# A router taken by token halves, with its products in column groups, two slots given new tenants, and three places reordered

## The chip, the cores and the metric

One core of one Trainium2 chip runs the kernel in one launch. The metric is device microseconds of one execution, the median of several. Before the change it is 545.25 us.

## The reference, cut to what matters

One encoder layer over 256 tokens of width 1024, batch 1, all in fp32:

```python
h = rmsnorm(x, g_mix)
rq, rk, rv, rg, nq, nk, nv, xq, gate_logits = split(h @ w_in)
y_ret = retention(rope(rq), rope(rk), rv, rg) @ w_ret_o
y_na  = neighbourhood_attention(nq, nk, nv, rpb) @ w_na_o
y_xa  = cross_attention(xq, rmsnorm(mem, g_mem) @ w_mem_kv) @ w_xa_o
x = x + (g_ret * y_ret + g_na * y_na + g_xa * y_xa) @ w_out
t = rmsnorm(x, g_ffn)
group  = top1(softmax(t @ w_router_group + b))          # 4 groups
expert = top2(softmax(t @ w_router_expert + b)[group])  # 4 experts in each
x = x + sum over the 2 chosen experts: weight * (silu(t @ w_gate) * (t @ w_up)) @ w_down
return rmsnorm(x, g_final)
```

There are 16 experts of hidden width 512. Each has 6.3 MB of weights, so their weights are most of what the kernel reads.

## The kernel before, in words

Tokens stand in two halves of 128 (index `a`), the width in eight blocks of 128 or two halves of 512 (index `n`). The big projections are three products each: a weight block is loaded raw, ScalarE casts it to a high part (L128) and VectorE subtracts to get a low part (L129), and TensorE adds hi*hi, hi*lo and lo*hi (L306 to L308 for token-major output, L288 to L290 for the transposed one, L874 to L876 in `wout`). The high and low parts live in the slots `h0` to `h4`. SyncE issues the loads in order; a load into a slot waits for the slot's last reader.

Up to the retention branch's output a scheduler sets the order of the work, except for instructions that `pin` keeps in program order. From there on (`tc.manual_schedule()`) the order is the program's.

Four stages matter here.

*The first row scaling.* `diag_of(col_x)` (L231 to L235) puts each token's factor on the diagonal of two 128x128 blocks on VectorE (L234). `row_of` (L237) multiplies that by ones on TensorE (L239) and copies it out (L241). The queries of the cross attention (`pair_T`, L396) read it.

*Rotation and neighbourhood attention.* `rope_T` (L538) multiplies the projection by cosines and sines and adds (L551), for two pairs of blocks. `na_probs` (L521) transposes the softmaxed scores (`flip`), then copies one half to SBUF on ScalarE (L524) and one on VectorE (L525). `na_out` (L528) multiplies these probabilities with the values (L533) on TensorE. `na_scores`, `na_probs` and `na_out` are called for four pairs of heads, between the projections for retention. Four GpSimd products (L582) that build the retention's decay matrix fall between the first two calls; ScalarE's exponentials (L581) feed them.

*The router*, from the second half of `wout`'s products to the first expert matmul. `x1_sum` (L883) adds the residual on VectorE, `x1_sq` squares it on ScalarE, `x1_T` (L892) transposes it, `x1_ev` (L895) copies that to SBUF. `logits` (L900) multiplies each transposed block, as the stationary operand, with 32 columns of `wr`. `seed` (L906) is a product of the identity with x1: it puts x1 into the four PSUM banks in which the experts' outputs are summed. `route` (L1011 to L1038) is a row of small VectorE operations: top group, top two experts, and `msk`, a 0/1 row of 16 for each token. Products with a triangle and with ones (L1054) count the tokens ahead of each token, `posm` (L1056, L1067) is a token's place in an expert's list, and `X` (L1108) compares that with 0 to 63 to make a 0/1 selection. `gather` (L1123) multiplies the normed x1, in a high part (`normed_hi`, L979) and a low part (`normed_lo`, L983), with `X`. The result is scaled into `xg` by ScalarE (L1146) and VectorE (L1150). `x1` and `xg` share slot `C1`, `x1_hi` is in `C2`. The two halves `a` go through this together: `route(0)` and `route(1)` are interleaved, and products follow when both are done.

*The experts*, in pairs: gate and up products (L1191) are written 64 columns wide, two experts side by side; then come the down products (L1210) and a scatter back to the tokens. `fetch(tag)` (L139) issues the next expert load of a fixed list into a slot that has come free.

Of the kernel before, what the change touches and what calls it, by code (L numbers as in the profile page):

```python
# [18 lines left out]
P = 128  # L19
# [11 lines left out]
def hybrid_encoder_kernel(  # L31
# [506 lines left out]
    def rope_T(tag, pts):  # L538
        hi, lo = [t.rearrange("p (c t) -> p c t", c=4) for t in pair(tag)]
        for b in range(2):  # L540
            cs = slice(2 * b, 2 * b + 2)
            u = by_row(cos, pts[b])
            v = small_tmp([P, 2, T])
            for d in (0, 64):
                V.tensor_tensor(
                    v[d : d + 64],
                    pts[b][64 - d : 128 - d],
                    sin[64 - d : 128 - d].unsqueeze(1).to_broadcast([64, 2, T]),
                    op=ALU.mult,
                )  # L550
            V.tensor_add(u, u, v)  # L551
            split(hi[:, cs], lo[:, cs], u)
        return hi, lo
# [16 lines left out]
    rk_hi, rk_lo = rope_T("C1", proj_T(units_T(W, C_RK, D), hT_hi, hT_lo))  # L570
    ps = na_probs(p)
# [192 lines left out]
    def expert_units():  # L764
# [39 lines left out]
        ("F", slot("F", [P, 4, 512])),  # L804
# [41 lines left out]
    for u in range(2):  # L846
# [15 lines left out]
        for _ in range(2 - u):  # L862
            lead_lo()
    A.activation(warm, mg[1][:, 1, 1, 511:512], AF.Exp)
# [3 lines left out]
    def wout(q, pts):  # L868
        w = halves.pop(0)
        for a in range(2):  # L870
            ts = slice(a * P, (a + 1) * P)
            for k in range(2):
                kk = 2 * q + k
                PE.matmul(pts[a], m_hi[kk // 4][:, kk % 4, ts], w[k][0], start=kk == 0, stop=False)  # L874
                PE.matmul(pts[a], m_hi[kk // 4][:, kk % 4, ts], w[k][1], start=False, stop=False)
                PE.matmul(pts[a], m_lo[kk // 4][:, kk % 4, ts], w[k][0], start=False, stop=kk == KT - 1)  # L876
        if not parts:
            hl_tags.remove(w[2])
            fetch(w[2])
# [22 lines left out]
    acc = [[None, None], [None, None]]  # L902

    def seed(base, a, n):
        acc[a][n] = acc[a][n] or pj([P, 512])
        PE.matmul(acc[a][n], ident, base[:, a, n * 512 : n * 512 + 512], start=True, stop=False)  # L906

    x1 = slot("C1", [P, 2, D])
    p0 = [pj([P, 512]) for _ in range(2)]
    for q in range(4):  # L910
        if q < 2:
            mt = mixed_T(1, q)
        wout(q, p0)
        if q < 2:
            mixed(1, q, mt)
        feed()
# [6 lines left out]
    rlog = [bank([P, 32]) for _ in range(2)]  # L923
    p1 = [pj([P, 512]) for _ in range(2)]
    xt = [bank([P, 4, P]) for _ in range(2)]
    x1T[0] = tmp([P, 4, 256])
    x1_sum(0, 0, p0)
    x1_sum(0, 1, p0)
    x1_sq(0, 0)
    x1_sq(0, 1)  # L930
    wout(0, p1)
    feed()
    wout(1, p1)
    fetch("A0")
    x1_T(0, 0, xt[0])
    x1_T(0, 1, xt[1])
    feed()
    x1_ev(0, 0, xt[0])
    x1_ev(0, 1, xt[1])
    wout(2, p1)  # L940
    logits(0, 0)
    logits(0, 1)
    feed()
    wout(3, p1)
    xt = [pj([P, 4, P]) for _ in range(2)]
    x1T[1] = tmp([P, 4, 256])
# [7 lines left out]
    x1_sum(1, 0, p1)  # L954
    fetch("E0")
    x1_T(1, 0, xt[0])
    x1_sq(1, 0)
    x1_ev(1, 0, xt[0])
    x1_sum(1, 1, p1)
    x1_rstd(0)  # L960
    x1_T(1, 1, xt[1])
    logits(1, 0)
    x1_sq(1, 1)
    x1_ev(1, 1, xt[1])
    logits(1, 1)
    x1_rstd(1)
    tx.close()
    tpx.close()
    fp = ctx.enter_context(tc.tile_pool(name="fp", bufs=1))
    for tag in ("T0", "T1"):  # L970
        home[tag] = fp
        fetch(tag)

    x1_hi = slot("C2", [P, 2, D], F32R)
# [12 lines left out]
    for a in range(2):  # L987
        for n in range(2):
            normed_hi(a, n)
            seed(x1, a, n)  # L990
    show("x1", x1)
# [19 lines left out]
    def route(a):  # L1011
        V.scalar_tensor_tensor(lgt[:, a, 0:20], rlog[a][:, :20], r2[:, a : a + 1], rb, op0=ALU.mult, op1=ALU.add)
        yield
        V.max(gval[:, a], lgt[:, a, 16:24])
        yield
# [3 lines left out]
        yield  # L1019
# [6 lines left out]
        yield  # L1026
        V.tensor_reduce(pad[:, a, 0:4], sel[:, a].rearrange("p g e -> p e g"), axis=AX.X, op=ALU.add)
        yield
        V.max(eval_[:, a], pad[:, a])
        yield  # L1030
        V.max_index(eidx[:, a], eval_[:, a], pad[:, a])
        yield
        for i in range(2):
            V.tensor_tensor(oh[:, i, a], io4, eidx[:, a, i : i + 1].to_broadcast([P, 4]), op=ALU.is_equal)
        yield
        V.tensor_add(m4[:, a], oh[:, 0, a], oh[:, 1, a])
        yield
        spread(msk, m4, a)  # L1038
        yield

    rt = [route(a) for a in range(2)]
    for i in range(16):
        if i < 11:
            next(rt[0])
        if i >= 5:
            next(rt[1])
    pp = bank([P, 3, 16])
    for o, pieces in (
        (pp[:, 0], ((tri, 0),)),
        (pp[:, 1], ((tri, 1), (ones, 0))),  # L1050
        (pp[:, 2], ((ones, 0), (ones, 1))),
    ):
        for i, (l, a) in enumerate(pieces):
            PE.matmul(o, l, msk[:, a], start=i == 0, stop=i == len(pieces) - 1)  # L1054
    posm = cp.tile([P, 2, 16], F32, name="posm")
    V.tensor_scalar(posm, msk, 1e6, -1e6, op0=ALU.mult, op1=ALU.add)  # L1056
    gneg = tiny(2, tag="gneg")
    V.tensor_scalar_mul(gneg, gval[:, :, 0], -1.0)
    gsum = tiny(2, tag="gsum")
# [3 lines left out]
    e21 = tiny(2, tag="e21")  # L1063
    V.tensor_sub(e21, eval_[:, :, 1], eval_[:, :, 0])
    A.activation(e21, e21, AF.Exp)
    A.activation(warm, e21[:, 0:1], AF.Silu)
    V.tensor_add(posm, posm, pp[:, 0:2])  # L1067
    cmax = tiny(1, tag="cmax")

    def counts():  # L1070
        V.tensor_reduce(cmax, pp[:, 2], axis=AX.X, op=ALU.max)

# [30 lines left out]
    counts()  # L1103

    def select(g):
        pd = slot("X", [P, 2, 4, SLOTS], F32R)
        for a in range(2):
            V.tensor_tensor(  # L1108
                pd[:, a],
                posm[:, a, 4 * g : 4 * g + 4].unsqueeze(2).to_broadcast([P, 4, SLOTS]),  # L1110
                iota.unsqueeze(1).to_broadcast([P, 4, SLOTS]),
                op=ALU.is_equal,
            )
        return pd

    def gather(pd, lead=False):
        pts = [bank([P, 2, 256]) for _ in range(4)]

        def part(u, x, first):
            for j in range(2):  # L1120
                ks = slice((2 * u + j) * P, (2 * u + j + 1) * P)
                for a in range(2):
                    PE.matmul(  # L1123
                        pts[u][:, j],
                        x[:, a, ks],
                        pd[:, a].rearrange("p e s -> p (e s)"),
                        start=first and j + a == 0,
                        stop=not first and j + a == 2,
                    )

        if lead:
            for u in range(4):
                part(u, x1_hi, True)
            for n in range(2):
                for a in range(2):
                    normed_lo(a, n)
        xg = slot("C1", [P, KT, 4, SLOTS])
        for u in range(4):
            pt = pts[u]
            if not lead:  # L1140
                part(u, x1_hi, True)
            part(u, x1_lo, False)
            if u % 2:
# [142 lines left out]
    def experts(pd, first, lead=False):  # L1286
# [19 lines left out]
        xg = gather(pd, lead)  # L1306
        for p in range(NP):
# [33 lines left out]
    pd0 = select(0)  # L1341
    experts(pd0, weights, True)
# [83 lines left out]
```

## Time and profile before

| | |
|---|---|
| median of 3 runs | 545.25 us (545.08 to 545.47) |
| the profiled execution | 545.44 us, its span 543.5 us |
| granted clock, mean | 0.994 of full speed |
| TensorE (PE) busy | 97% of the span |
| VectorE (DVE), ScalarE (ACT), GpSimd (POOL) | 49%, 42%, 3% |
| moved by DMA | 159.91 MB, mean 294 GB/s |

Times in rows are us from the span's start. A timeline row reads: start, length, engine, line, operation, output <- input, tile used by a matmul, shape, count of instructions in the row, and in square brackets the idle time before it with what ended it. Matmuls overlap their ends: the step from one to the next is the cost, the length is not (a 512-column record of L874 to L876 is 0.39 us long and follows the one before by 0.23 us). An fp32 matmul can be two records.

### The profile page before, as it was taken

Reading aid. Unit: us, or ns where it says so; the run is one execution under the profiler, and the core shown is the slowest. Engines: PE = TensorE matmul, PEld = TensorE weight load, DVE = VectorE, ACT = ScalarE, POOL = GpSimd, SP = SyncE. Lnnn points to the kernel's source line nnn. Section 1 sums busy time; section 2 is a strip of 40 time slices with the busy share of each in tenths; the row PEclk is TensorE's granted clock in tenths of the full one; section 3 lists DMA queues with packets and bytes.
Section 4 is the critical chain, followed back from the end, with each engine's and each line's share of the span. In section 5 each row is a group of like instructions: output and inputs, shape, how many; then the busy total and the mean of one; then the engine's idle time right before and its main releaser. Section 6 shows DMA issues by size and latency. Waiting matters only on the chain. (4 is left out here: it accounts for less than half of the span.)

```text
span 543.5 us, 7482 instructions
## 1 busy us (share of the span) xinstructions
PE 528.5 (97%) x2912; PEld 359.9 (66%) x2912; DVE 264.3 (49%) x461; ACT 229.0 (42%) x378; POOL 18.5 (3%) x21
## 2 busy tenths in 40 slices
PE   8999999999999999999999999999999999999992
PEld 6999899967778888888888863353435343534340
DVE  6598798995657768384566171130112111210122
ACT  6775566698654464544535261121111111111123
POOL 0005000040000000000000000000000000000000
PEclk9999999999999999999999999999999999999997
DMA  8987778045445799739983799999999999999962
GB/s 302 390 316 233 224 147 256 17 156 163 148 154 189 235 334 301 257 103 403 354 318 151 275 344 330 416 406 418 406 414 409 409 413 407 416 406 418 406 242 81
DMA packets 89815, 159.91 MB, mean 294 GB/s; under 512 B 13104, under 2 KB 27824, under 8 KB 89776
## 3 DMA queue, kind: packets, MB, share of 16 engines
q1 hardware_dynamic: 89056, 158.80, 80.1%
q10 hardware_dynamic: 720, 0.58, 0.3%
q8 instruction: 25, 0.41, 0.3%
q14 instruction: 14, 0.11, 0.1%
HBM read 158.32 MB, written 1.05 MB: 293 GB/s over the span
## 5 line engine op out<-in xcount | busy, mean ns | idle before, releaser
L129 DVE TENSOR_TENSOR h<-r,h 128x1024 fp32r<-128x1024 f32 x58 | 71.2, 1239 | 31.6 <-ACT h L128 31.2
L128 ACT CAST h<-r 128x1024 fp32r<-128x1024 f32 x58 | 60.2, 1048 | 23.4 <-PE pj L308 12.5
L306 PE MATMUL pj<-h,A 128*128 128x512 f32 x160 | 63.1, 394 | 0.0
L308 PE MATMUL pj<-h,A 128*128 128x512 f32 x160 | 62.7, 392 | 0.0
L307 PE MATMUL pj<-h,A 128*128 128x512 f32 x160 | 62.6, 391 | 0.0
L1199 DVE TENSOR_TENSOR gs<-gs,b 64x512 f32<-64x512 f32 x16 | 11.1, 691 | 87.1 <-ACT gs L1198 87.1
L288 PE MATMUL pj<-A,h 128*128 128x256 f32 x160 | 45.7, 286 | 0.0
L290 PE MATMUL pj<-A,h 128*128 128x256 f32 x160 | 45.5, 284 | 0.0
L289 PE MATMUL pj<-A,h 128*128 128x256 f32 x160 | 45.3, 283 | 0.0
L308 PEld LDWEIGHTS pj<-h,A 128*128 128x128 f32 x160 | 30.1, 188 | 6.9 <-issue 0.8
L306 PEld LDWEIGHTS pj<-h,A 128*128 128x128 f32 x160 | 30.1, 188 | 6.7 <-issue 0.4
L307 PEld LDWEIGHTS pj<-h,A 128*128 128x128 f32 x160 | 30.1, 188 | 6.3 <-DVE h L129 0.4
L1230 DVE SCALAR_TENSOR_TENSOR os<-b,c,os 128x512 fp32r<-128x512 f32 x16 | 12.0, 751 | 41.9 <-ACT os L1229 41.0
L1198 ACT ACTIVATE gs<-b 64x512 f32<-64x512 f32 x16 | 9.4, 588 | 51.8 <-PE b L1191 51.8
L288 PEld LDWEIGHTS pj<-A,h 128*128 128x128 f32 x160 | 30.7, 192 | 0.1
L290 PEld LDWEIGHTS pj<-A,h 128*128 128x128 f32 x160 | 30.7, 192 | 0.1
L289 PEld LDWEIGHTS pj<-A,h 128*128 128x128 f32 x160 | 30.7, 192 | 0.1
L129 DVE TENSOR_TENSOR h<-G,h 128x1024 fp32r<-128x1024 f32 x18 | 24.1, 1346 | 10.3 <-ACT h L128 9.8
L1229 ACT ACTIVATE os<-b,c 128x512 fp32r<-128x512 f32 x16 | 11.0, 687 | 40.6 <-PE b L1210 39.7
L1191 PE MATMUL b<-h,C 128*64 128x512 f32 x104 | 24.0, 592 | 0.0
L128 ACT CAST h<-G 128x1024 fp32r<-128x1024 f32 x18 | 18.8, 1049 | 10.6 <-PE pj L308 9.3
L1210 PE MATMUL b<-h,hh 128*64 128x512 f32 x64 | 21.3, 592 | 0.0
(327 smaller groups left out, 1029.3 us busy)
## 6 DMA issues: line engine op xcount, KB each, us to landing
r<-in_w_in_dram SPq DMA_DIRECT2D x20, 1024.0 KB, 5.4
h<-in_w_exp_down_dram SPq DMA_DIRECT2D x10, 1024.0 KB, 11.5
h<-in_w_exp_gate_dram SPq DMA_DIRECT2D x13, 512.0 KB, 11.0
h<-in_w_exp_up_dram SPq DMA_DIRECT2D x13, 512.0 KB, 11.1
r<-in_w_exp_down_dram SPq DMA_DIRECT2D x6, 1024.0 KB, 11.6
A<-in_w_exp_down_dram SPq DMA_DIRECT2D x5, 1024.0 KB, 11.4
r<-in_w_exp_gate_dram SPq DMA_DIRECT2D x9, 512.0 KB, 10.2
r<-in_w_exp_up_dram SPq DMA_DIRECT2D x9, 512.0 KB, 10.3
```

What stands on the lines that cost most here:

```text
L128: pin(A.copy(hi, part))
L129: pin(V.tensor_sub(lo, part, hi.bitcast(F32)))
L288: PE.matmul(pt, whi[:, cs], thi[:, k], start=k == 0, stop=False)
L289: PE.matmul(pt, whi[:, cs], tlo[:, k], start=False, stop=False)
L290: PE.matmul(pt, wlo[:, cs], thi[:, k], start=False, stop=k == kn - 1)
L306: PE.matmul(pts[a], thi[:, kk, ts], whi, start=first, stop=False)
L307: PE.matmul(pts[a], thi[:, kk, ts], wlo, start=False, stop=False)
L308: PE.matmul(pts[a], tlo[:, kk, ts], whi, start=False, stop=last)
L1191: PE.matmul(pt[c * 64 : c * 64 + 64], xg[:, k, p % 2 * 2 + i], w[:, 2 * c + j], start=k == 0, stop=k == KT - 1)
L1199: V.tensor_mul(gs[i * 64 : i * 64 + 64], gs[64:128], pt[64:128])
L1210: PE.matmul(pts[n][i * 64 : i * 64 + 64], hh[:, 2 * u + k], ws[i][1][:, k, ns], start=u + k == 0, stop=u + k == 2)
L1230: V.scalar_tensor_tensor(o[:, 1], pt, c, o[:, 0].bitcast(F32), op0=ALU.mult, op1=ALU.subtract)
```

## The change

It does five things. (1) `diag_of(col_x)` is called before the neighbourhood queries' weights are split, no longer inside the call of `row_of`. (2) `rope_T` of the keys takes a function that is called ahead of its last addition: the copies of the first `na_probs` come before that addition. (3) The router works on token half 0 while half 1's `wout` products still run. Its logits turn the operands around: `wr` (32 columns) is stationary, four blocks go to four groups of 32 output partitions, ScalarE copies the 128 rows (`sheaves`) and a product with `four` (four stacked 32x32 identities) adds the four groups. Seeds and the parts of the first gather are written out one by one between the waits; seeds are 256 columns wide. `x1_sq`, `normed_hi` and `normed_lo` come earlier; the three small products of the counts are split. The pieces of the gather's results that go to ScalarE and to VectorE are swapped for this first gather. (4) `x1` and the first `xg` live in slot `F`, `x1_hi` in a half-weight slot. `C1` and `C2` take the two expert loads that `F` and that half-weight slot took, right after the retention's output. (5) The order of VectorE's and ScalarE's work follows from (1) to (3).

```diff
+    diag_x = diag_of(col_x)
     nq_u = units_T(W, C_NQ, D, pin)
-    row_x = row_of("q", diag_of(col_x))
+    row_x = row_of("q", diag_x)
...
-            V.tensor_add(u, u, v)
+            if b and mid:
+                mid()
+                pin(V.tensor_add(u, u, v))
+            else:
+                V.tensor_add(u, u, v)
...
-    rk_hi, rk_lo = rope_T("C1", proj_T(units_T(W, C_RK, D), hT_hi, hT_lo))
-    ps = na_probs(p)
+    rk_hi, rk_lo = rope_T("C1", proj_T(units_T(W, C_RK, D), hT_hi, hT_lo), lambda: probs.append(na_probs(p)))
+    (ps,) = probs
...
-        ("F", slot("F", [P, 4, 512])),
+        ("", slot("F", [P, 4, 512])),
...
+    for tag in ("C1", "C2"):
+        fetch(tag)
     A.activation(warm, mg[1][:, 1, 1, 511:512], AF.Exp)
...
-            PE.matmul(rlog[a], x1T[n][:, j, a * P : (a + 1) * P], wr[:, k], start=k == 0, stop=k == KT - 1)
+            PE.matmul(
+                sheaf[a][32 * j : 32 * j + 32],
+                wr[:, k],
+                x1T[n][:, j, a * P : (a + 1) * P],
+                start=not n,
+                stop=bool(n),
+            )
+    def bound(a):
+        A.copy(sheaves[:, a], sheaf[a])
+        PE.matmul(rlog[a], sheaves[:, a], four, start=True, stop=True)
-    x1 = slot("C1", [P, 2, D])
+    x1 = slot("F", [P, 2, D])
...
+    wout(1, p1, ws[1], 0)
+    for a in range(2):
+        x1_T(0, a, xt[a])
+        x1_ev(0, a, xt[a])
+    wout(2, p1, ws[2], 0)
+    wout(3, p1, ws[3], 0)
+    for a in range(2):
+        logits(0, a)
+    x1_sum(1, 0, p1)
+    x1_sq(1, 0)
+    x1_rstd(0)
+    wout(1, p1, ws[1], 1)
+    used(ws[1])
+    fetch("A0")
+    x1_T(1, 0, xt[2])
+    x1_ev(1, 0, xt[2])
+    for n in range(2):
+        normed_hi(0, n)
+        normed_lo(0, n)
+    wout(2, p1, ws[2], 1)
+    used(ws[2])
+    logits(1, 0)
+    wout(3, p1, ws[3], 1, (0,))
+    bound(0)
+    wout(3, p1, ws[3], 1, (1,))
+    used(ws[3])
+    fetch("E0")
+    rt = [route(a) for a in range(2)]
+    next(rt[0])
+    x1_sum(1, 1, p1)
+    x1_sq(1, 1)
+    next(rt[0])
+    x1_rstd(1)
+    seed(x1, 0, 0)
+    x1_T(1, 1, xt[1])
+    x1_ev(1, 1, xt[1])
+    seed(x1, 1, 0)
+    logits(1, 1)
+    PE.matmul(pp[0], tri, msk[:, 0], start=True, stop=True)
+    pd0 = slot("X", [P, 2, 4, SLOTS], F32R)
+    settled(0)
+    chosen(pd0, 0, 0)
+    bound(1)
...
+    for u in range(3):
+        for x in (x1_hi, x1_lo):
+            part(lead[u], u, x, pd0, 0, x is x1_hi, False)
+    for n in range(2):
+        normed_hi(1, n)
+    for _ in range(2):
+        next(rt[1])
+    seed(x1, 0, 1)
...
+    settled(1)
+    counts()
+    chosen(pd0, 0, 1)
+    seed(x1, 1, 1, (0,))
+    part(spare, 3, x1_hi, pd0, 0, True, False)
+    part(spare, 3, x1_lo, pd0, 0, False, False)
+    for u in range(4):
+        part(lead[u], u, x1_hi, pd0, 1, False, False)
...
+    for n in range(2):
+        normed_lo(1, n)
+    for u in range(4):
+        part(lead[u], u, x1_lo, pd0, 1, False, True)
+    seed(x1, 1, 1, (1,))
```

`settled(a)` is the place of a half's tokens, `chosen(pd, g, a)` the 0/1 selection of a half, and `part` one block pair of the gather for one half and one of the two parts.

How the order moves is seen in three places. ScalarE's queue around the second call of `na_out`, before (`h_198` is the high part of a weight block for the retention's values, `t_170` the probabilities that the second `na_out` reads, `G_154` and `C_140` parts of the values and the keys, `t_151` the softmaxed scores):

```order
L128 CAST h_182_1518<-r_181_1516 128x1024
L354 ACTIVATE t_151_1350,sm_1349<-t_148_1342,mx_1343 128x256 x4
L316 ACTIVATE G_154_1368<-pj_1403,col_239 128x512
L358 ACTIVATE t_151_1350<-t_151_1350,rs_1355 128x256 x4
L128 CAST h_183_1521<-r_181_1516 128x1024
L316 ACTIVATE G_154_1368<-pj_1404,col_239 128x512
L524 COPY t_170_1466<-at_1457 128x512
L128 CAST h_198_1633<-r_197_1631 128x1024
L313 CAST B_108_994<-at_1501 128x256
```

And in the changed kernel:

```order
L354 ACTIVATE t_151_1350,sm_1349<-t_148_1342,mx_1343 128x256 x4
L128 CAST h_182_1518<-r_181_1516 128x1024
L358 ACTIVATE t_151_1350<-t_151_1350,rs_1355 128x256 x4
L316 ACTIVATE G_154_1368<-pj_1403,col_239 128x512
L128 CAST h_183_1521<-r_181_1516 128x1024
L316 ACTIVATE G_154_1368<-pj_1404,col_239 128x512
L128 CAST h_198_1633<-r_197_1631 128x1024
L525 COPY t_170_1466<-at_1457 128x512
L313 CAST B_108_994<-at_1501 128x256
```

The copy of the probabilities (L524 before, L525 now) now stands behind the cast of `h_198`. On VectorE the same holds: the subtraction of `h_198` now stands ahead of the other half's copy, where it stood ten instructions behind it. In the changed kernel's TensorE queue the second `na_out` stands four projection matmuls later.

TensorE's queue behind the last `wout` product, before (`C_359` is x1, `pj_2946` and `pj_2947` its transposes, `b_2855` and `b_2856` the logits of the halves):

```order
L892 MATMUL pj_2946<-ident,C_359_2771 128x128 x4
L892 MATMUL pj_2947<-ident,C_359_2771 128x128 x4
L900 MATMUL b_2855<-wr,t_385_2948 128x32 x4
L900 MATMUL b_2856<-wr,t_385_2948 128x32 x4
L906 MATMUL pj_2997<-C_359_2771,ident 128x512
L906 MATMUL pj_3000<-C_359_2771,ident 128x512
L906 MATMUL pj_3003<-C_359_2771,ident 128x512
L906 MATMUL pj_3006<-C_359_2771,ident 128x512
```

And in the changed kernel, where `F_2776` is x1, `X_3025` the selection, `h_382` and `E_378` the high and low part, and `b_2857` to `b_2860` the four banks `lead`:

```order
L955 MATMUL pj_2777<-F_2776,ident 128x256 x2
L899 MATMUL b_2858<-ident,F_2776 128x128 x4
L955 MATMUL pj_2778<-F_2776,ident 128x256 x2
L907 MATMUL b_2860<-t_377_2870,wr 32x128 x4
L1097 LDWEIGHTS tri
L1097 MATMUL b_2857<-msk,tri 128x16
L917 MATMUL b_2860<-four,sheaves 128x32
L1036 MATMUL b_2857<-X_3025,h_382_2904 128x256 x2
L1036 MATMUL b_2857<-X_3025,E_378_2872 128x256 x2
L1036 MATMUL b_2858<-X_3025,h_382_2904 128x256 x2
L1036 MATMUL b_2858<-X_3025,E_378_2872 128x256 x2
L1036 MATMUL b_2859<-X_3025,h_382_2904 128x256 x2
```

Seeds, the transposes of the last quarter of x1, its logits, the first count and parts of the gather now take turns; before, all seeds stood ahead of the counts, and the gather behind them. The last half-seed (`seed(x1, 1, 1, (1,))`) is TensorE's last product ahead of the experts, and the scaling of `xg`, which overwrites x1's slot, waits for it.

SyncE's queue of expert loads behind the first eight, before:

```order
L152 DMA B_480_3481<-in_w_exp_down_dram 128x2x1024
L152 DMA F_3487<-in_w_exp_down_dram 128x2x1024
L152 DMA h_483_3496<-in_w_exp_gate_dram 128x2x512
L152 DMA h_483_3496<-in_w_exp_up_dram 128x2x512
```

And in the changed kernel:

```order
L152 DMA B_469_3485<-in_w_exp_down_dram 128x2x1024
L152 DMA C_470_3491<-in_w_exp_down_dram 128x2x1024
L152 DMA C_472_3500<-in_w_exp_gate_dram 128x2x512
L152 DMA C_472_3500<-in_w_exp_up_dram 128x2x512
```

The list of loads is the same. The fourth of a row of down loads goes to `C` in place of `F`, and the gate and up load behind it to `C` in place of a half-weight slot; both are issued when the retention's output is done, where the second was issued in the middle of the router before.

## Rows read from the trace of the kernel before

**Rows 1.** The page's busy times: us, share of the span, instructions

```profile
PE 528.5 (97%) x2912; PEld 359.9 (66%) x2912; DVE 264.3 (49%) x461; ACT 229.0 (42%) x378; POOL 18.5 (3%) x21
```

**Rows 2.** TensorE's waits: line, releaser, us in total, times, longest

```profile
PE at L533 <- DVE t L525: 1.6, 3, 1.0
```

**Rows 3.** Busy us of PE, PEld, DVE, ACT, POOL; clock; DMA share, GB/s

```profile
285.00:300.00 15.00, 15.00 (x72) 12.40 (x71) 10.50 (x13) 8.70 (x11) 0.00 (x0) 1.00 0.38 140
325.00:330.00 5.00, 5.00 (x26) 1.68 (x24) 0.00 (x0) 0.42 (x2) 0.00 (x0) 1.00 0.62 214
330.00:524.00 194.00, 194.00 (x1014) 80.15 (x1012) 31.01 (x65) 32.56 (x61) 0.00 (x0) 1.00 1.04 409
524.00:528.00 4.00, 4.00 (x20) 1.79 (x17) 1.98 (x3) 1.55 (x3) 0.00 (x0) 1.00 0.14 53
```

**Rows 4.** Timeline, TensorE then VectorE, around the first row scaling

```profile
30.13 0.28 PE L290 MATMUL pj<-A,h 128*128 128x256 f32 x1
30.49 0.70 PE L239 MATMUL at<-t,ones_f 128*128 128x256 f32 x2
...
25.29 4.76 DVE L129 TENSOR_TENSOR h<-r,h 128x1024 fp32r<-128x1024 f32 x4 [0.91 <-ACT h L128]
29.96 0.47 DVE L234 TENSOR_SCALAR t<-ident,col 128x128 f32<-128x128 f32 x2
```

**Rows 5.** Timeline: PE, VectorE, ScalarE, GpSimd around the first na_out

```profile
115.26 1.08 PE L533 MATMUL at<-t,E 128*64 128x256 f32 x8 [1.04 <-DVE t L525]
...
112.82 1.78 DVE L551 TENSOR_TENSOR t<-t,t 128x512 f32<-128x512 f32 x1
114.53 0.68 DVE L525 COPY t<-at 128x512 f32<-128x512 f32 x1
...
112.97 0.56 ACT L524 COPY t<-at 128x512 f32<-128x512 f32 x1
...
112.52 3.21 POOL L582 TENSOR_TENSOR C<-C,t 128x512 f32<-128x512 f32 x2 [63.46 <-ACT t L581]
```

**Rows 6.** Timeline: ScalarE, VectorE, TensorE around the second na_out

```profile
125.70 0.57 ACT L524 COPY t<-at 128x512 f32<-128x512 f32 x1
126.17 1.06 ACT L128 CAST h<-r 128x1024 fp32r<-128x1024 f32 x1
...
127.05 0.68 DVE L525 COPY t<-at 128x512 f32<-128x512 f32 x1
...
127.79 1.08 PE L533 MATMUL at<-t,E 128*64 128x256 f32 x8 [0.36 <-DVE t L525]
```

**Rows 7.** Timeline of TensorE from w_out's last product to the first expert

```profile
307.81 1.87 PE L900 MATMUL b<-wr,t 128*128 128x32 f32 x16
312.13 0.40 PE L876 MATMUL pj<-h,E 128*128 128x512 f32 x1
313.31 0.66 PE L892 MATMUL pj<-ident,C 128*128 128x128 f32 x4 [0.35 <-DVE C L883]
313.81 2.01 PE L900 MATMUL b<-wr,t 128*128 128x32 f32 x16
315.65 3.68 PE L906 MATMUL pj<-C,ident 128*128 128x512 f32 x8
320.27 2.36 PE L1123 MATMUL b<-X,C 128*128 128x256 f32 x16 [0.83 <-DVE X L1108]
322.47 2.08 PE L1123 MATMUL b<-X,E 128*128 128x256 f32 x16
324.48 1.94 PE L1191 MATMUL b<-B,C 128*64 128x512 f32 x8
```

**Rows 8.** Timeline of VectorE in the same stretch

```profile
314.90 0.24 DVE L1012 SCALAR_TENSOR_TENSOR lgt<-b,r,rb 128x20 f32<-128x20 f32 x1 [0.50 <-PE b L900]
319.70 0.76 DVE L1108 TENSOR_TENSOR X<-posm,iota 128x256 fp32r<-128x256 f32 x2
323.22 0.69 DVE L1150 TENSOR_TENSOR C<-b,gt 128x512 f32<-128x512 f32 x1
```

More of the change, by code (lines that the diff above doesn't have):

```diff
@@ L863, in hybrid_encoder_kernel, with wout, used @@
             lead_lo()
+    for tag in ("C1", "C2"):
+        fetch(tag)
     A.activation(warm, mg[1][:, 1, 1, 511:512], AF.Exp)
     x1T = {}
[L868 to L879, printed above, removed]
+    def wout(q, pts, w, a, ks=(0, 1)):
+        ts = slice(a * P, (a + 1) * P)
+        for k in ks:
+            kk = 2 * q + k
+            PE.matmul(pts[a], m_hi[kk // 4][:, kk % 4, ts], w[k][0], start=kk == 0, stop=False)
+            PE.matmul(pts[a], m_hi[kk // 4][:, kk % 4, ts], w[k][1], start=False, stop=False)
+            PE.matmul(pts[a], m_lo[kk // 4][:, kk % 4, ts], w[k][0], start=False, stop=kk == KT - 1)
+    def used(w):
+        hl_tags.remove(w[2])
+        fetch(w[2])
     def x1_sum(n, a, pts):
@@ L912, in hybrid_encoder_kernel @@
             mt = mixed_T(1, q)
-        wout(q, p0)
+        w = halves.pop(0)
+        for a in range(2):
+            wout(q, p0, w, a)
         if q < 2:
             mixed(1, q, mt)
+        if not parts:
+            used(w)
         feed()
@@ L985, in normed_lo @@
         )
[L987 to L991, printed above, removed]
     gval = cp.tile([P, 2, 8], F32, name="gval")
@@ new lines, in part, with counts @@
+    def part(pt, u, x, pd, a, first, last):
+        pt = pt.rearrange("p (j c) -> p j c", j=2)
+        for j in range(2):
+            k = 2 * u + j
+            PE.matmul(
+                pt[:, j],
+                x[:, a, k * P : (k + 1) * P],
+                pd[:, a].rearrange("p e s -> p (e s)"),
+                start=first and not j,
+                stop=last and j == 1,
+            )
+    cmax = tiny(1, tag="cmax")
+    def counts():
+        V.tensor_reduce(cmax, pp[2], axis=AX.X, op=ALU.max)
@@ new lines, in hybrid_encoder_kernel @@
+    for a in range(2):
+        x1_sum(0, a, p0)
+        x1_sq(0, a)
+    ws = [halves.pop(0)]
+    for a in range(2):
+        wout(0, p1, ws[0], a)
+    hl_tags.remove(ws[0][2])
+    x1_hi = slot(ws[0][2], [P, 2, D], F32R)
+    feed()
+    ws += halves
+    wout(1, p1, ws[1], 0)
+    for a in range(2):
+        x1_T(0, a, xt[a])
+        x1_ev(0, a, xt[a])
+    wout(2, p1, ws[2], 0)
+    wout(3, p1, ws[3], 0)
+    for a in range(2):
+        logits(0, a)
+    x1_sum(1, 0, p1)
+    x1_sq(1, 0)
@@ new lines, in hybrid_encoder_kernel @@
+    for n in range(2):
[3 more added lines that the diff above has]
+    seed(x1, 0, 1)
+    for o, pieces in ((pp[1], ((tri, 1), (ones, 0))), (pp[2], ((ones, 0), (ones, 1)))):
+        for i, (l, a) in enumerate(pieces):
+            PE.matmul(o, l, msk[:, a], start=i == 0, stop=i == 1)
+    settled(1)
[6 more added lines that the diff above has]
+        part(lead[u], u, x1_hi, pd0, 1, False, False)
@@ L1107, in select, with gather @@
         for a in range(2):
[L1108 to L1113, printed above, removed]
-        return pd
[L1116 to L1137, printed above, removed]
+            chosen(pd, g, a)
+        return pd
+    def gather(pd, pts=None):
+        done = pts
+        pts = pts or [bank([P, 512]) for _ in range(4)]
+        xg = slot("F", [P, KT, 4, SLOTS])
         for u in range(4):
             pt = pts[u]
[L1140 to L1143, printed above, removed]
+            for x in () if done else (x1_hi, x1_lo):
+                for a in range(2):
+                    part(pt, u, x, pd, a, x is x1_hi and a == 0, x is x1_lo and a == 1)
+            pt = pt.rearrange("p (j c) -> p j c", j=2)
+            if bool(u % 2) != bool(done):
                 for j in range(2):
@@ L1339, in experts @@
         finish(1)
-    pd0 = select(0)
-    experts(pd0, weights, True)
+    experts(pd0, weights, lead)
     run.close()
```

123 lines of the change are left out of this document (43 added, 80 removed).

## The prediction

> **What bounds the kernel now.** I read the page's busy times first. TensorE works in 528.5 of 543.5 us [rows 1]; the other engines are half idle, and the memory queues have spare time except in the experts' stage. So a microsecond comes off only where TensorE does less, or where it stands still. The table of waits by releaser says how little it stands still: at the second matmul of neighbourhood attention (L533) it waits three times, 1.6 in all, 1.0 at most, for VectorE's copy of the probabilities [rows 2]; in the router, the gather waits 0.83 for the selection X [rows 7]. The table by stretches shows the second limit: from 330 to 524 DMA is full at 409 GB/s, yet TensorE is busy for 194.00 of 194.00 [rows 3]. At 524 to 528 the DMA share is 0.14, about 0.6 us of work, while four more microseconds of matmuls and then the tail follow. I take from this that the last weights arrive some 3 us ahead of their use: the experts follow TensorE now, and would follow DMA if TensorE came more than about 3 us earlier. So what the change wins ahead of 324.48, up to that, should reach the end whole.
>
> The sum is made against the profiled execution, 545.44; it lies 0.19 over the median of 545.25. A measurement of this kernel tells about 0.2%, or 1.1 us, from no change.
>
> **The first row scaling.** The last matmul before L239 starts at 30.13, and a 256-column record follows the one before by 0.12 there; L239 starts at 30.49, so TensorE lost about 0.24 [rows 4]. What it waits for are the two diagonal blocks on VectorE, 0.47, at 29.96, and these stand behind four subtractions of 4.76. The change puts them ahead of the four, into an idle stretch of 0.91 that the row of the four shows. The subtractions then start on time, and L239, 12 matmuls earlier in the queue, finds its input. I take **-0.24**; ends 0 (the time turns up as a wait for the low parts instead) and -0.3.
>
> **The probabilities, first call.** TensorE stands still 1.04 ahead of L533 at 115.26. VectorE's copy (114.53, 0.68 long) stands behind the rotation's addition L551, which began at 112.82 and took 1.78 while GpSimd ran its two products from 112.52, 3.21 [rows 5]. The change lets the copy go first. It also waits for ScalarE's copy of the other half, 112.97 and 0.56 long, so it can run from about 113.6 to 114.3, and L533 starts there: -0.95. The addition then falls wholly beside GpSimd.
>
> **The probabilities, second call.** Here the change takes back. Before, ScalarE's copy ran at 125.70 and the cast of the next weight block behind it, at 126.17, 1.06 long; VectorE's copy ran at 127.05 and L533 at 127.79, after a wait of 0.36 [rows 6]. In the new order that cast stands ahead of ScalarE's copy and its subtraction ahead of VectorE's. A subtraction is 4.76 / 4 = 1.19 [rows 4], of which I count 1.15. If ScalarE's chain ahead of it (exponentials, norms, gates) is where it was, VectorE's copy starts at 127.05 + 1.15 = 128.2 and L533 at 128.9. ScalarE's fourth exponential for GpSimd now precedes more of that chain and waits for GpSimd's second product, which ends at 112.52 + 3.21 = 115.73; I add 0.2: 129.1. L533 stands four matmuls of 0.23 later in the new queue, so on an unchanged schedule it would start at 127.79 + 0.91 = 128.70. The two calls together come to **+0.4**: the 0.95 is used up, and a little more. Ends: -1.3 if the copy is never late (both waits of 1.04 and 0.36 gone, less 0.1), +0.85 if the chain on ScalarE slips by 0.45 more.
>
> A rule bears on this. L551's row shows 1.78 for an addition of 128x512 [rows 5], where another VectorE operation of that size, with GpSimd idle, takes 0.69 [rows 8]. The Trainium skill (SBUF — State Buffer, Who interferes with whom) says that a VectorE instruction with two inputs in SBUF contends with a GpSimd instruction that reads SBUF, and that the one that issues second blocks until the other ends. The row agrees at least in that it was held up. By that rule alone the addition waits to 115.73 in the new order, the chain slips to the late end, and the sum of this change is 0.45 higher than mine.
>
> **The router: TensorE's work.** After the last `wout` product (312.13 + 0.23 = 312.37) TensorE needed 12.11 to the first expert product at 324.48 [rows 7]. The gather's two rows step by 2.20 and 324.48 - 322.47 = 2.01, so 4.21. One set of transposes steps by 313.81 - 313.31 = 0.50. Logits change: the second set's 16 records step by 315.65 - 313.81 = 1.84 at a length of 2.01, so 0.17 of a length is overlap, and the first set's 1.87 steps by 1.70: eight products, 0.85 for a half's four. The seeds' 3.68 is 3.52 by the same allowance. Seeds and gather keep their work. A product in a group of 32 output columns has no row. A fp32 product with 128 moving columns alone should take a quarter of a seed's 3.52 / 4 = 0.88, so 0.22; four that do not overlap make 0.88, four that do make 0.22. Nearest are the experts' products: eight records of 512 moving columns in 64-column pairs at L1191 are 1.94 long, about half of the seeds' eight records of 512 at 3.68. Two groups do overlap. I take 0.43 for four, between the ends.
>
> Ahead of `wout`'s end the new order carries the logits of two quarters (-0.85), but also the third quarter's transposes (+0.50) and logits (+0.43), and a product with `four` (+0.2): its end comes at about 312.65. Behind it stand 3.52 of seeds, 4.21 of gather, one set of transposes 0.5, logits 0.43, `four` 0.2 and 0.25 of small count products: 9.1. The stretch before is 12.11 less the waits of 0.35 and 0.83 that its rows show, so 10.9.
>
> **The router: waits.** Before, VectorE came from the first operation of `route` at 314.90 to X at 319.70, both halves interleaved and the counts between them; X is 0.38 a half [rows 8]. A half alone I put at 2.5 up to `msk`, about half of that, since each small operation waits for the one before. Half 0 can start at 312.2, but x1's last addition (0.69) is put between its third and fourth operation, so `msk` is there at 315.35, the place and X at 316.4. TensorE's seeds and transposes fill to 315.05, logits, count and `four` to some 315.6: wait 0.85. Half 1 starts with `four` at 316.3 and its X is done at 320.2: between them 12 records of gather (1.65), two seeds' worth and parts; wait 0.4. The last half-seed ends at 323.1, and only then may `xg` be written into x1's slot: VectorE 0.69 [rows 8], and a hand-over: the experts begin at 324.0. So **-0.45**. Ends: -1.6 if TensorE only has its work and the final scaling (312.65 + 9.1 + 1.1 = 322.85), +1.1 if the column groups do not overlap (below).
>
> **Slots.** Two loads move to 285 to 300, where the DMA share is 0.38, and hide there. Others are issued later: seven loads of 1.05 MB follow from about 308.7, 7.3 MB, 18 us at 409 GB/s, so to 326.7. Before, DMA had idle time there as well: share 0.62 in 325 to 330 [rows 3]. So the stream that fills DMA from 326 on starts from the same point, and I price this at 0; ends 0 and +0.5. If the cover of 3 us were gone it would all be on the path.
>
> **Sum.** -0.24 + 0.4 - 0.45 = -0.29: 545.15 against the profiled 545.44, **545.0** against the median.
>
> **The rivals.** (a) *TensorE's work decides the router.* My waits of 0.85, 0.4 and 0.9 (323.1 to 324.0) are by hand, and each could be filled by a neighbour, since the new order spreads the seeds as fillers. Then the router gives -1.6 and the first scaling -0.24; with the probabilities at 0 it is -1.84, 543.4; without any late copy 542.2. For it: 1.8 less work on the engine that is busy for 97%. Against it: VectorE's chain for half 1 cannot start before the logits of half 1. (b) *Slower: the four groups take turns.* At 0.88 for four products instead of 0.43, `wout` ends 3 x 0.45 = 1.35 later, and the last set delays half 1's chain by another 0.2: router +1.1, sum -0.24 + 0.4 + 1.1 = +1.26, 546.5. It decides at more than about 0.8 for four. The overlap seen at L1191 speaks against it. The Trainium skill (TensorEngine Tiling (Array Packing), Key Properties) adds that a change of tiling mode drains TensorE; six such changes stand in the new router. Rows 7 do not show a drain where L1123 hands over to L1191, with 2.01 for the last sixteen records against 2.20 for the sixteen before. (c) *Slower by the second copy*, +0.85 there and nothing won in the router: +0.6, 545.9, inside the same band.
>
> **How the numbers follow.** Forecast, with ends of about 0.9 to either side: 0.43. (a) 0.33; (b) 0.14; (c) 0.10. Faster by over 0.2% (under 544.2) comes from (a) and a tail of the forecast: 0.38; slower (over 546.3) from (b), a part of (c) with the late ends and the forecast's other tail: 0.21; the rest 0.41. The range 543.0 to 546.7 leaves out the far ends of (a) and of (b). The forecast's own range is 544.1 to 545.9.
>
> **What would show it.** In the profile after: no wait at the first L534 and one of 1.5 or more at the second; L239's counterpart without a gap; L907's four products stepping 0.4 in all (0.22 or 0.88 in the rivals); the end of the last `wout` product at 312.65; the first expert product near 324.0; TensorE busy without a gap from there to the last loads. Wrong would be a DMA wait of TensorE behind 330, or an expert start ahead of 323 or after 325.

## The result: 0.75% slower, and the profile after

The changed kernel takes 549.5 us in the median of four runs (549.18 to 549.67), the kernel before 545.31 in the same comparison: a ratio of 1.0075, interval 1.0063 to 1.0087. The profiled execution took 549.67, its span is 547.7. The time lies outside my range, on the side to which I had given the smallest chance.

TensorE is as busy as before, for 528.6 us against 528.5 [rows 1]; what grew is the time in which it stands still. From the changed kernel's page, the busy time by engine:

```profile
PE 528.6 (97%) x2924; PEld 360.0 (66%) x2924; DVE 264.9 (48%) x462; ACT 230.3 (42%) x384; POOL 18.2 (3%) x21
```

The table of waits of the changed kernel for TensorE (who waited, for whom, us in total, times, longest) is the answer to [rows 2]:

```profile
PE b L1255 <- DMA r<-in_w_exp_down_dram: 2.9, 2, 1.5
PE at L534 <- DVE t L526: 1.4, 2, 1.2
PE at L259 <- POOL ident masks.py:199: 1.4, 1, 1.4
PE at L224 <- POOL E L215: 1.1, 1, 1.1
PE b L1236 <- ACT F L1191: 0.8, 1, 0.8
PE b L1266 <- DMA A<-in_w_exp_down_dram: 0.5, 1, 0.5
PE b L917 <- ACT sheaves L916: 0.3, 1, 0.3
```

Two rows wait for expert weights, which before never happened, and a third (L224, the squares of the cross attention's memory) waits for work that hangs on an early load. The table by stretches of the changed kernel, to be read beside [rows 3] (last two numbers: DMA share and GB/s):

```profile
330.00:524.00 194.00, 191.08 (x992) 78.97 (x990) 30.32 (x64) 31.21 (x58) 0.00 (x0) 1.00 1.04 397
524.00:528.00 4.00, 4.00 (x22) 1.38 (x20) 0.92 (x2) 1.55 (x3) 0.00 (x0) 1.00 1.05 386
```

In the experts' stage DMA is as full as before, at a share of 1.04, and moves 397 GB/s instead of 409. In the same 194 us the DMA view counts, before:

```profile
DMA packets 34431, 79.32 MB, mean 409 GB/s; under 512 B 1988, under 2 KB 1988, under 8 KB 34421
## 3 DMA queue, kind: packets, MB, share of 16 engines
q1 hardware_dynamic: 34421, 79.18, 103.8%
```

and in the changed kernel:

```profile
DMA packets 33313, 76.96 MB, mean 397 GB/s; under 512 B 1941, under 2 KB 1941, under 8 KB 33303
...
q1 hardware_dynamic: 33303, 76.82, 104.2%
```

The packets carry the same 2.3 KB each in the mean, and they take longer (share times 16 engines times the stretch, by the number of packets): 1.038 x 16 x 194 us / 34421 = 93.6 ns before, 1.042 x 16 x 194 / 33303 = 97.1 ns after, 3.7% more. 2.36 MB less arrive, worth 5.8 us at 409 GB/s. With 3 us of cover that cannot be hidden. Where it comes out is the end of the changed kernel's TensorE timeline (columns as in the section on time and profile):

```profile
504.91 0.64 PE L1255 MATMUL b<-r,hh 128*64 128x512 f32 x1 [1.41 <-DMA r<-in_w_exp_down_dram]
...
510.04 3.65 PE L1255 MATMUL b<-r,hh 128*64 128x512 f32 x14 [1.48 <-DMA r<-in_w_exp_down_dram]
...
529.08 1.94 PE L1266 MATMUL b<-A,hh 128*64 128x512 f32 x8 [0.48 <-DMA A<-in_w_exp_down_dram]
...
534.85 2.38 PE L1298 MATMUL pj<-T,T 128*128 128x512 f32 x8
```

Its counterpart before is the last row of TensorE there:

```profile
530.62 2.38 PE L1253 MATMUL pj<-T,T 128*128 128x512 f32 x8
```

The last products start 4.23 later, although the experts began earlier: the router's end in the changed kernel, beside [rows 7]:

```profile
306.76 0.64 PE L907 MATMUL b<-t,wr 128*32 128x128 f32 x16
307.34 0.50 PE L880 MATMUL pj<-h,A 128*128 128x512 f32 x1
...
312.62 0.39 PE L882 MATMUL pj<-h,E 128*128 128x512 f32 x1
...
316.06 0.41 PE L917 MATMUL b<-four,sheaves 128*128 128x32 f32 x2 [0.27 <-ACT sheaves L916]
316.51 0.51 PE L1036 MATMUL b<-X,h 128*128 128x256 f32 x2
...
322.23 0.59 PE L955 MATMUL pj<-F,ident 128*128 128x256 f32 x2
323.65 0.65 PE L1236 MATMUL b<-B,F 128*64 128x512 f32 x2 [0.83 <-ACT F L1191]
```

The first expert product starts at 323.65, 0.83 ahead of [rows 7]. From there to the last products the stage is 4.23 + 0.83 = 5.06 longer. So the question is why a full DMA became slower.

### The profile page after: what moved, and what is told of

It is laid out like the page before. It is cut to its first block, busy times and chain, and to the rows that moved or that the text cites. A ratio compares the mean times of both kernels' runs of the same rounds, so it can differ in the third digit from the quotient of the medians.

```text
span 547.7 us, 7511 instructions
## 1 busy us (share of the span) xinstructions
PE 528.6 (97%) x2924; PEld 360.0 (66%) x2924; DVE 264.9 (48%) x462; ACT 230.3 (42%) x384; POOL 18.2 (3%) x21
## 3 DMA queue, kind: packets, MB, share of 16 engines
HBM read 158.32 MB, written 1.05 MB: 291 GB/s over the span
## 5 line engine op out<-in xcount | busy, mean ns | idle before, releaser
L129 DVE TENSOR_TENSOR h<-r,h 128x1024 fp32r<-128x1024 f32 x58 | 70.1, 1222 | 29.7 <-ACT h L128 28.6
L1236 PE MATMUL b<-h,F 128*64 128x512 f32 x88 | 20.6, 592 | 0.0
```

The lines of the kernel that those rows point to most:

```text
L129: pin(V.tensor_sub(lo, part, hi.bitcast(F32)))
L1236: PE.matmul(pt[c * 64 : c * 64 + 64], xg[:, k, p % 2 * 2 + i], w[:, 2 * c + j], start=k == 0, stop=k == KT - 1)
```

## The experiments

Eleven edited kernels and the kernel before once more ran in three groups; the kernel before, run beside each group, had medians of 545.28 to 545.31.

**First group: which part of the change?** The first theory: the two slots with new tenants (part 4) make loads later or bunch them. The rival: it lies in some other part. *slots_as_before* is the changed kernel with the slots of before; *slots_alone* is the kernel before with part 4 alone; *early_alone* has parts 1 and 2 alone; *before_again* is the kernel before, unchanged.

```diff
 slots_as_before, against the changed kernel
-        ("", slot("F", [P, 4, 512])),
+        ("F", slot("F", [P, 4, 512])),
-    for tag in ("C1", "C2"):
-        fetch(tag)
-    x1 = slot("F", [P, 2, D])
+    x1 = slot("C1", [P, 2, D])
...
 early_alone, against the kernel before
+    diag_x = diag_of(col_x)
     nq_u = units_T(W, C_NQ, D, pin)
-    row_x = row_of("q", diag_of(col_x))
+    row_x = row_of("q", diag_x)
...
+            if b and mid:
+                mid()
+                pin(V.tensor_add(u, u, v))
```

(*slots_alone* is the first of these edits the other way round, made to the kernel before.)

> The changed kernel with the slots of before: F takes its load at about 292, the half-weight slot its load at about 302, x1 and xg are in C1, x1_hi in C2; the two early loads into C1 and C2 are gone. Theory S (the slots: loads that are issued only at 309 leave DMA idle from 292 to 309, and the experts then wait for weights): DMA moves 409 GB/s in the experts' stage again, TensorE waits for DMA under 0.5 us, and the gain of the router (first expert product 0.8 us earlier) reaches the end: 544.3 to 545.0. Theory R (the transfer rate: packets take longer than before for a reason outside the slots): the rate stays near 397 GB/s, and the time near 549.

> The kernel before with the slots of the changed kernel alone: C1 and C2 take their loads at about 288, x1 and xg are in F, x1_hi in a half-weight slot, nothing goes into F at 292 or into the half-weight slot at 302. Theory S: as late as the changed kernel or later, 548.5 to 550.5, with waits for DMA behind 480. Theory R: 545 to 546 at 409 GB/s.

> The kernel before with the earlier diagonal blocks and the copies ahead of the keys' last addition alone. Theory S: 545.2 to 546.0, since the trace of the changed kernel stands 0.2 us later than before at the start of w_out's second half; 409 GB/s in the experts' stage. Theory R, if the cause were here: 548 to 550 at about 397 GB/s.

> The kernel before, unchanged, profiled on the same chip as the three others. Theory S: 545.1 to 545.6, packets of 2048 B as short as in the first trace, 409 GB/s from 330 to 524. Theory R, if the rate is a matter of the chip or the hour: about 397 GB/s, and some waits for DMA at the end.

Measured: slots_as_before 549.75 (ratio 1.0079, interval 1.0063 to 1.0096), as slow as the change and with the same 397 GB/s; slots_alone 545.29 (0.9998, 0.9988 to 1.0007) at 410 GB/s; early_alone 544.59 (0.9989, 0.998 to 0.9999) at 409 GB/s; before_again 545.87 in one execution. The theory of the slots falls: part 4 costs nothing and undoing it returns nothing. What is left is the router. Its order would have to slow down single packets 200 us later, which no run had excluded so far. But the router also brings two new constants, `sheaves` of 1024 bytes in each partition and `four` of 128. They stand in the pool ahead of all weight slots. By the addresses in the built program every slot, from a multiple of 512 bytes, is moved by 1152 = 4 x 256 + 128 bytes: `r0` from 28160 to 29312.

**Second group: where the slots begin.** Theory: loads into slots off some power of two are slower; then the change with an aligned `four` is fast, and the kernel before with slots shifted by an unused constant is slow. Rival: the router's order does it.

```diff
 after_aligned, against the changed kernel
-    four = cp.tile([P, 32], F32, name="four")
+    four = cp.tile([P, 128], F32, name="four")[:, :32]
 before_shifted_128, against the kernel before
     r2 = cp.tile([P, 2], F32, name="r2")
+    filler = cp.tile([P, 32], F32, name="filler")
+    G.memset(filler, 0.0)
```

*before_shifted_64* has a filler of 16 columns (64 bytes) instead; *slots_before_aligned* is slots_as_before with the wider `four`.

> The changed kernel with one edit: the constant four takes 512 B of a partition in place of 128, so that the two new constants together shift every weight slot by 1536 B and not by 1152; the slots start at multiples of 512 B again, as before the change. Nothing else differs. Theory A (the place of the slots in a partition slows DMA packets): packets of 2048 B take 84 ns each again, DMA moves 409 GB/s from 330 to 524, no wait of TensorE for DMA, and 543.4 to 544.6. Theory B (something in the router's work slows DMA): still 397 GB/s and 549 to 550.

> The kernel before with an unused constant of 128 B of a partition (written once by GpSimd in the router), which puts every weight slot 128 B behind a multiple of 512, as the change does. Theory A: packets lengthen as in the changed kernel, about 397 GB/s, waits of TensorE for DMA at the end; the last transfer lands some 5 us later against 3 us of cover, so 546.5 to 549.5. Theory B: 545.0 to 545.8.

> As the run with 128 B, with 64 B. Theory A, if any place off a multiple of 512 B costs the same: 546.5 to 549.5; if the cost goes with the distance, less or more than with 128 B. Theory B: 545.0 to 545.8.

> The changed kernel with the slots of before and the weight slots at multiples of 512 B. Theory A: 543.4 to 544.6, the same as with the new slots, if these are worth nothing with a cover of 3 us; theory B: 549 to 550.

Measured: after_aligned **543.49** (0.9966, 0.9952 to 0.9979): one constant of unchanged use, made 384 bytes wider, is worth 6 us. before_shifted_128: 551.79 (1.0113, 1.0098 to 1.0128). before_shifted_64: 553.99 (1.0151, 1.0135 to 1.0166). slots_before_aligned: 543.37 (0.9964, 0.9951 to 0.9978). The row of the experts' stretch in after_aligned:

```profile
330.00:524.00 194.00, 194.00 (x1014) 80.30 (x1012) 32.05 (x67) 32.87 (x62) 0.00 (x0) 1.00 1.04 409
```

in before_shifted_128:

```profile
330.00:524.00 194.00, 191.47 (x996) 79.01 (x994) 30.06 (x63) 30.91 (x57) 0.00 (x0) 1.00 1.04 394
```

and in before_shifted_64:

```profile
330.00:524.00 194.00, 190.43 (x966) 77.88 (x964) 30.00 (x62) 30.44 (x56) 0.00 (x0) 1.00 1.04 392
```

The same share in all three, at 409, 394 and 392 GB/s. before_shifted_128 has the order of before and shows the waits of the changed kernel:

```profile
PE b L1212 <- DMA r<-in_w_exp_down_dram: 2.5, 2, 1.5
PE at L239 <- DVE t L234: 2.0, 1, 2.0
...
PE b L1223 <- DMA A<-in_w_exp_down_dram: 0.5, 1, 0.5
```

The rival falls: after_aligned has the new order and is fast, before_shifted_128 has the old one and is slow. The second of these rows also shows that the start of the kernel becomes longer: L239's wait, 0.24 in [rows 4], is 2.0 here. From 2 to 30 us DMA has a share of 1.05 in all of these kernels, and moves 374 GB/s before, 375 in after_aligned, 353 in the changed kernel, 350 and 349 with the slots shifted by 128 and 64 bytes.

**Third group: which multiple, how much of it, and what the rest of the change is worth.** *before_shifted_256* has a filler of 64 columns (256 bytes). *before_half_shifted* puts the filler of 128 bytes between the slots, so that twelve of the 21 (`E0`, `r0` to `r2`, `A0`, `A1`, `h0` to `h4`, `G0`) stay where they were and nine are moved. *aligned_without_rope* is after_aligned with part 2 undone. *aligned_copies_pinned* tries to mend the late second copy: after_aligned, with the second `na_probs` and the projection for the first gate chunk kept in program order.

```diff
 before_half_shifted, against the kernel before
     xq_u = units_T(W, C_XQ, D, parts=2)
+    filler = sp.tile([P, 32], F32, tag="filler", name="filler")
+    G.memset(filler, 0.0)
     x_n = slot("F", [P, 2, D])
 aligned_copies_pinned, against after_aligned
-        A.copy(ps[:, 0], pt[:, 0])
-        V.tensor_copy(ps[:, 1], pt[:, 1])
+        pin(A.copy(ps[:, 0], pt[:, 0]))
+        pin(V.tensor_copy(ps[:, 1], pt[:, 1]))
...
-        pts = proj_N(units(W, c_gate + n * 512, D), hT_hi, hT_lo)
+        pts = proj_N(units(W, c_gate + n * 512, D, pin), hT_hi, hT_lo)
```

> The kernel before with an unused constant of 256 B, so that the weight slots start 256 B behind a multiple of 512. If the boundary that counts is 512 B, as slow as with 64 and 128 B: 550 to 555 and 390 to 398 GB/s from 330 to 524. If 256 B is enough: 545.0 to 545.9 and 409 GB/s.

> The kernel before with a gap of 128 B between slot G0 and slot F: E0, r0 to r2, A0, A1, h0 to h4 and G0 stay at multiples of 512 B, F, E1, E2, C0 to C2, G1, B0, B1, X stand 128 B behind one. If each packet pays for its own slot's place, the rate lies about halfway, 402 to 405 GB/s, and the time at 546 to 548; if one shifted slot among those in flight slows all, 394 to 398 GB/s and 550 to 552; if only r0 to r2 and h0 to h4, the slots of the first stages, count, 409 GB/s and 545.0 to 545.9.

> The aligned changed kernel with the copies behind the keys' last addition again (part 2 undone). By the traces the wait of 1.04 ahead of the first na_out went and one of 1.2 at the second came: 543.3 to 543.7, the same as the aligned kernel within 0.2%. By the prediction's step (+0.4 for part 2) it is 0.4 faster, 543.1; if part 2 were worth its 0.95, 544.4.

> The aligned changed kernel with the copies of the second na_probs and the weight blocks of the first gate chunk kept in program order, so that no weight block of that chunk is cast ahead of the copies. If the second wait of 1.2 is due to that cast and goes without a new wait: 542.2 to 542.8. If later blocks now come late, because the order behind it moves too: 543.5 to 545.

Measured: before_shifted_256 545.65 (1.0004, 0.9995 to 1.0014), no change, with this row:

```profile
330.00:524.00 194.00, 194.00 (x1014) 80.15 (x1012) 31.02 (x65) 32.46 (x61) 0.00 (x0) 1.00 1.04 409
```

So neither the filler nor a shift as such costs anything; a multiple of 256 bytes is enough. before_half_shifted: 546.85 (1.0027, 1.0016 to 1.0038), between the two. It is only partly in proportion: its experts' stretch moves 407 GB/s, 2 less than before, where half of 15 would be 7; its first expert product starts at 325.92 against 324.60 in before_shifted_256, and that is nearly the whole loss. Three rows of before_half_shifted, the whole stretch and two parts of it, show that its loss comes in bursts:

```profile
330.00:524.00 194.00, 194.00 (x1013) 79.92 (x1008) 31.02 (x65) 31.80 (x59) 0.00 (x0) 1.00 1.04 407
...
489.00:494.50 5.50, 5.50 (x34) 2.86 (x32) 0.33 (x2) 0.37 (x1) 0.00 (x0) 1.00 1.05 388
414.60:427.40 12.80, 12.80 (x76) 6.73 (x74) 2.10 (x4) 2.86 (x6) 0.00 (x0) 1.00 1.05 407
```

The second part is filled by loads into slots that stayed, the first by loads into moved ones. The traces' records of single packets say more. From 330 to 524, packets of 2048 bytes take 84 ns in the kernel before; longer than 85 ns are 1% of them there, 11% in before_half_shifted, 60% in before_shifted_128 and 63% in the changed kernel. They come in batches of sixteen loads, 256 packets to a load, so they can be counted off in the order in which the loads are issued. In before_half_shifted, nearly all of the longer ones then belong to loads into moved slots, and the rest to the load just behind a series of these. But they do not come at once. In the last two series of eight loads into moved slots, at most 4% of the packets of each of the first three loads are longer, of the fourth's 61 and 72%, of each later load's 70 to 81%. A series of four ends just there. This is also why the slots that lie 128 bytes off in the kernel before show no loss: `T`'s are filled four loads in a row, and in the stretch the fourth alone has longer packets to speak of (27 and 8% of them). So a long series of loads into shifted slots pays, a short one hardly. What lets the first three pass is open.

aligned_without_rope: 543.21 (0.9966, 0.9953 to 0.9979), the same time as after_aligned. aligned_copies_pinned missed: 548.84 (1.006, 1.0047 to 1.0074) at a full 411 GB/s. Its waits:

```profile
PE at L534 <- DVE t L526: 3.0, 2, 1.8
PE pj L306 <- ACT h L128: 1.4, 1, 1.4
```

Pinning left the second `na_out` late, made the third wait 1.81 instead of 0.20, and gave the projection behind it a new wait of 1.42. That is 3.0 of the 4.8 by which its first expert product starts behind after_aligned's (327.11 against 322.33). Most of the rest is TensorE's clock. Its rows, and the stretch around them (clock 0.74):

```profile
144.10 1.63 PE L306 MATMUL pj<-h,A 128*128 128x512 f32 x3 [1.42 <-ACT h L128]
145.53 0.63 PE L307 MATMUL pj<-h,A 128*128 128x512 f32 x1
145.96 0.63 PE L308 MATMUL pj<-h,A 128*128 128x512 f32 x1
...
145.00:150.00 5.00, 5.00 (x19) 3.91 (x18) 2.17 (x4) 5.00 (x12) 0.00 (x0) 0.74 0.13 30
```

Behind the two waits the products step by 0.43 in place of 0.23, up to 147.62: the granted clock had fallen to the lower of its two levels, 1.2 GHz. Eight products cost 1.7 more. The executions of this kernel differ with it, from 546.76 at a mean granted clock of 0.993 to 549.16 at 0.987.

## Why the prediction was wrong, point by point

**The step that failed** is the price of the loads: "I price this at 0", with 409 GB/s carried over from the kernel before ("18 us at 409 GB/s"). For the new tenants themselves the 0 was right: undoing part 4 changes nothing, with shifted slots or with aligned ones. What had no term was the rate. I took 409 for a property of the kernel that the change could not touch, and looked at when loads are issued, never at where they land, though the change puts two constants ahead of every slot. The runs put the price of the shifted slots at 549.5 - 543.49 = **6.0**. Where it stands is seen in four rows: L224 in the changed kernel and in after_aligned, then after_aligned's first expert product and its last products:

```profile
47.27 0.60 PE L224 MATMUL at<-ones_f,E 128*128 128x1 f32 x4 [1.07 <-POOL E L215]
...
46.05 0.50 PE L224 MATMUL at<-ones_f,E 128*128 128x1 f32 x4
...
322.33 1.94 PE L1236 MATMUL b<-B,F 128*64 128x512 f32 x8 [0.83 <-ACT F L1191]
...
528.45 2.38 PE L1298 MATMUL pj<-T,T 128*128 128x512 f32 x8
```

The last products lie 534.85 - 528.45 = 6.40 apart. Of that, 1.32 stands at the first expert product (323.65 against 322.33), 1.22 of it since L224, and 5.08 behind it. The experts' products stay 1.32 apart until 498, and the lag grows only at the three waits for weights. The table puts these waits at 3.4; the other 1.7 by which the lag grows there was not separated. The bytes explain most of the 5.08: 2.36 MB missing from 330 to 524 and 0.42 MB up to 330 (the rates of the stretches from 285, summed) are 6.8 us at 409 GB/s; less the cover of 3, plus 0.83 by which the changed kernel's experts start ahead of [rows 7], makes 4.6, against the 5.06 by which the stage is longer than before. So the cover was sized about rightly, and I had even written that without it a delay "would all be on the path".

**With the slots aligned, the kernel takes 543.49, where rival (a) had 543.4**, but that is partly luck: (a) had -1.6 in the router and -0.24 ahead of it, and the rows show about -1.1 in each. First expert products start at 324.48 before, at 322.33 in after_aligned, and here in early_alone:

```profile
323.41 1.94 PE L1197 MATMUL b<-B,C 128*64 128x512 f32 x8
```

What is won ahead of the experts reaches the end whole, as I assumed: after_aligned's first expert product is 2.15 ahead of before's, its last products, at 528.45, 2.17. By parts:

- *The first row scaling, -0.24*: right in sign, too small. No kernel with the edit waits at L239. L224, before and in early_alone:

```profile
47.11 0.61 PE L224 MATMUL at<-ones_f,E 128*128 128x1 f32 x4
...
45.94 0.61 PE L224 MATMUL at<-ones_f,E 128*128 128x1 f32 x4
```

  It starts 1.2 sooner. L239's wait gives 0.24 of that, or 0.69 by before_again's trace, so executions differ there; the weight load of L224 waited 0.3 for GpSimd before and no longer does. The remainder was not separated. In medians early_alone is 0.69 faster.
- *The probabilities, +0.4*: the mechanism was right, the sum 0.4 too high, because the second copy came 0.9 later and not 1.35. The two calls in after_aligned:

```profile
113.12 1.08 PE L534 MATMUL at<-t,E 128*64 128x256 f32 x8
127.59 1.08 PE L534 MATMUL at<-t,E 128*64 128x256 f32 x8 [1.23 <-DVE t L526]
```

and in aligned_without_rope, with the old order:

```profile
114.13 1.08 PE L534 MATMUL at<-t,E 128*64 128x256 f32 x8 [1.05 <-DVE t L526]
126.66 1.08 PE L534 MATMUL at<-t,E 128*64 128x256 f32 x8 [0.36 <-DVE t L526]
```

  The first wait goes and a second of 1.23 comes. The second call starts 127.59 - 126.66 = 0.93 later for 0.91 of matmuls that now precede it: net nothing, and the third call starts at 141.31 in both. ScalarE's chain did not slip by the late end's 0.45. The rule weighed there I had misapplied, as a wait for the end of two GpSimd products. After_aligned, VectorE and GpSimd (all four products, then the first two), and the first product of the kernel before:

```profile
112.98 1.68 DVE L554 TENSOR_TENSOR t<-t,t 128x512 f32<-128x512 f32 x1
...
111.34 5.74 POOL L588 TENSOR_TENSOR C<-C,t 128x512 f32<-128x512 f32 x4 [62.32 <-ACT t L587]
111.34 2.77 POOL L588 TENSOR_TENSOR C<-C,t 128x512 f32<-128x512 f32 x2 [62.32 <-ACT t L587]
...
112.52 1.53 POOL L582 TENSOR_TENSOR C<-C,t 128x512 f32<-128x512 f32 x1 [63.46 <-ACT t L581]
```

  The addition is stretched to 1.68, but it ends at 114.66, while GpSimd's four products go on to 117.08. It ends 0.55 behind the one product that was running when it began (111.34 + 2.77 = 114.11). Before, it ends at 114.60 [rows 5], again 0.55 behind the running product (112.52 + 1.53 = 114.05). So the rows fit a wait for a single product, as far as GpSimd's rough times go, and not for the stream.
- *The router, -0.45*: it gave -1.08 (first expert product 323.41 in early_alone, 322.33 in after_aligned). The end of `wout` came as counted: 0.24 later than in early_alone, 0.28 predicted. Behind it I had 9.2 of work and hand-overs, and waits of 0.85, 0.4 and 0.9; the rows show waits of 0.27, none and 0.83, and 9.7 of work (323.65 - 312.85 less the waits). So the waits that I set by hand were 1.05 too long, and the work 0.5 too short. `route(0)` came when I said, X at 316.45 against 316.4 in the changed kernel:

```profile
316.03 0.42 DVE L1025 TENSOR_TENSOR X<-posm,iota 128x256 fp32r<-128x256 f32 x1
```

  But TensorE had work up to 316.51 and waited only 0.27 there, for `sheaves`. The four products with 32 output columns step by (307.34 - 306.76) / 2 = 0.29 where I took 0.43, and 0.22 if they overlap fully.
- *Rival (b), columns in turns*: wrong, by the same rows. Where the products' shape changes, the steps into and out of L907's group are 0.32 and 0.34 against 0.23, so no long drain shows there.
- *Rival (c), the second copy*: the wait came, without the slip.
- *The test that I had named*, "a DMA wait of TensorE behind 330", is what the trace shows; the prediction named no cause for it beyond loads that are issued late.

## What to carry to other kernels

When a change adds or resizes a constant, look at where everything allocated behind it now begins: a small tile that left every slot 128 bytes off cost this kernel 6 us. Size the small tiles ahead of the slots of large loads so that these begin at multiples of 256 bytes. And where DMA's share is full, read GB/s at that share, not the share: the share was 1.04 in every kernel here, fast or slow.

## What the runs showed of the hardware

With all weight slots 128 or 64 bytes off a multiple of 256 in SBUF, the experts' loads run at 394 to 397 and at 392 GB/s, and with the slots at multiples of 256 at 409 to 411, with the same loads at the same full share. In a series of loads into shifted slots the first three keep their packet times: of the fourth's packets of 2048 bytes 61 and 72% take longer than 85 ns, of the first three's at most 4% (before_half_shifted). I had not expected the address in SBUF to matter at all. The Trainium skill (DMA: Bandwidth & Descriptors, How a descriptor splits into AXI transactions) says that a transaction must start at an address that is a multiple of 256 bytes, and that a descriptor which does not start there costs additional beats. It says this of what is read; here it is the place written that was moved. The boundary agrees: a shift of 256 costs nothing here. The order of the two offsets does not: by that section's count, an estimate, a start 64 bytes off needs no more beats than one 128 off, yet it was the slower. That packets lengthen because of such beats is not shown.

The best versions are after_aligned, slots_before_aligned and aligned_without_rope, at 543.2 to 543.5 us: 0.34 to 0.36% under the kernel before, and 1.1% under the change as it was made.
